# Two more input units of the second and third feed-forward blocks as seven half-size products, with the token sums, the modulation dots and their buffers moved to make room

## The chip, the cores and the metric

One core of one Trainium2 chip runs the whole program. The metric is the device time of one execution in microseconds (us), median over runs. TensorE (PE) multiplies matrices, with its weight loads shown on a row of their own (PEld); VectorE (DVE) and ScalarE (ACT) do the elementwise work; SyncE (SP) issues the loads from memory (DMA). Each engine works through its own list of instructions in the order in which the list stands, and waits at an instruction whose data or buffer isn't ready.

## The reference, cut to what matters

A two-layer model on 256 latent and 256 context tokens (512 in all), width 1024. Each layer is: half feed-forward block (FFN), mixer (attention in layer 0, mLSTM in layer 1), half FFN. Scale, shift and gate of each block come from a vector of conditions:

```python
mod = split(silu(c) @ ada_w[i] + ada_b[i], 9)      # once with c, once with c_ctx
def half_ffn(h, shift, scale, gate, w_in, w_out, g, b):
    xm = h * (1 + scale) + shift
    a, u = split(xm @ w_in, 2)                     # 1024 -> 2 x 2816
    y = (silu(a) * u) @ w_out                      # 2816 -> 1024
    return layer_norm(alpha * h + 0.5 * gate * y, g, b)
```

All of it is in 32-bit floating point.

## The kernel before, in words

**Products.** A product of two fp32 numbers is made of three matmuls on operands that are cut in a high and a low part (`mm3`, L241): high·high, high·low, low·high. The cut is `split`: ACT casts the high part (L225), DVE subtracts it from the whole to leave the low part (L230). Weights arrive whole by DMA (512 KB a tile of 128x1024, line L210, three buffers called raw) and are split into one of seven buffers, each a pair of high and low.

**FFNs.** There are four. The first stands before attention, the second after it, the third right after the second, the last after mLSTM. The first three go through `ffn`: the 2816 inner columns are 22 units of 128, in two halves of 11. In each half the input units come first (`unit_in`: 8 blocks of width, both a and u, three matmuls of 512 tokens each, so 48 matmuls), then the 8 output rows (`unit_out`: 11 units by three matmuls of 512 tokens, 33 in all), whose result DVE adds onto h (L713). Units 0 to 3 are done for the two halves of the tokens apart (lead units); so are the last four rows of the second half (tail).

**Fast units.** In the second and third FFN the second half's units 11 to 21 use a Strassen-like scheme (`fast_in`): a product of 2x2 blocks by seven half-size products in place of eight. The weight blocks of a unit are a11, a21 (first tile) and a12, a22 (second tile); the weight sums are s1 = a21 + a22, s2 = s1 - a11 and so on (four DVE additions and subtractions on 128x512, L636, then splits). The token blocks are the lower and upper half of the width by latent and context tokens; their sums are made once by `fast_sums` and overwrite the context part of the operand in place. The seven products (each 4 blocks by three matmuls of 256 tokens, so 84 matmuls a unit) are a11, a12, s1, s2, a22, s4, s3 in the order of the code; ACT copies partial results out of PSUM in between (L661 to L668), DVE combines them (L670, L674, L675), ACT applies silu (L671).

**Side work.** The vectors mod are dots of silu(c) with the columns of ada_w. DVE does them beside the matmuls: one piece is a tile of 128x1024 (512 KB) and one instruction for each of two condition vectors (`ada_dot`, L350). A call after each unit or row first does the dots of pieces that were loaded at the call before, then loads new ones. Layer normalisation leaves a scaling of h to be finished beside the units (`residual`, L563 and L564). In the program before, 56 pieces are done in the first FFN; the rest in the units 0 to 10, in the first rows and in the second half's rows of the second and third FFN. The token sums stand beside rows 4 and 5 of the first half, when the buffers of the dots have been closed to make room; silu(c) is loaded and computed again after unit 21.

**Order.** A scheduler gives each engine its list when the kernel is built; what stands where is read from that list.

Of the kernel before, what the change touches and what calls it, by code (L numbers as in the profile page):

```python
# [9 lines left out]
F32 = mybir.dt.float32  # L10
# [4 lines left out]
ALU = mybir.AluOpType  # L15
# [18 lines left out]
SH = 16  # L34
SHM = 48
SHR = 56
# [19 lines left out]
LEAD = 4  # L56
# [6 lines left out]
S1B = 5  # L63
# [18 lines left out]
FAFTER = 2  # L82
# [7 lines left out]
SUMSAT = 4  # L90
FLIP = 56
PIECES = 4
DOTS = {
    1: {**{("in", j): 2 for j in range(11)}, **{("out", 0, d): 2 if d < 2 else 1 for d in range(4)}, **{("out", 1, d): 1 for d in range(4)}},
    2: {**{("in", j): 2 for j in range(4)}, **{("in", j): 3 if j < 9 else 2 for j in range(4, 11)}, **{("out", 0, d): 2 if d < 3 else 0 for d in range(4)},
        **{("out", 1, d): 2 if d < 3 else 1 for d in range(4)}},
}
# [75 lines left out]
class Body:  # L173
    def __init__(self, ctx, tc, a, out):
        self.tc, self.nc, self.a, self.out = tc, tc.nc, a, out
        self.n = 0
        self.sp = ctx.enter_context(tc.tile_pool(name="sp", bufs=1))
        self.pp = ctx.enter_context(tc.tile_pool(name="pp", bufs=1, space=PSUM))
        self.later, self.running = [], []
        self.fence = {}  # L180
        self.fine = False

        self.nraw, self.spare = 0, None

# [104 lines left out]
    def silu_c(self):  # L289

        pool = ExitStack()
        self.n += 1
        p = pool.enter_context(self.tc.tile_pool(name=f"cp{self.n}", bufs=1, side="right"))
        self.cp = p
        self.cb = self.t([P, 2, D], pool=p)
        return pool
# [5 lines left out]
    def silu_all(self):  # L302
        pool = self.silu_c()
        self.silu_load()
        self.silu()
        return pool
# [285 lines left out]
    def fast_operands(self, st):  # L592

        n = ND // 2 * TL
        x = self.t([P, 6 * n], F32R, pool=st)
        self.t([P, FLIP], pool=st)
        self.made = [[x[:, (2 * i + p) * n : (2 * i + p + 1) * n].rearrange("p (k f) -> p k f", f=TL) for p in range(2)] for i in range(3)]

    def fast_sums(self, i):
# [5 lines left out]
        def at(ks, g):  # L605
            return self.xh[:, ks, g[0] : g[1]], self.xl[:, ks, g[0] : g[1]]

        def whole(ks, g):
            o = self.tmp().rearrange("p (k f) -> p k f", k=2)
            h, l = at(ks, g)  # L610
            V.tensor_tensor(out=o, in0=h.bitcast(F32), in1=l.bitcast(F32), op=ALU.add)
            return o

        a, b = whole(lo, LAT), whole(lo, CTX)
        V.tensor_tensor(out=a, in0=a, in1=b, op=ALU.subtract)
        self.split(a, *at(lo, CTX))
# [3 lines left out]
        V.scalar_tensor_tensor(a, a, -1.0, c, ALU.mult, ALU.subtract)  # L620
        self.split(a, *made(0))
        d = whole(up, LAT)
        V.scalar_tensor_tensor(d, a, -1.0, d, ALU.mult, ALU.subtract)
        self.split(d, *made(2))

    def fast_in(self, j, w_in, st):

        nc, V, S = self.nc, self.nc.vector, self.nc.scalar
        half = 4 * P
        t4 = self.made[2]  # L630
# [5 lines left out]
        add = lambda o, x, y: V.tensor_tensor(out=o, in0=x, in1=y, op=ALU.add)  # L636
        ws = [self.pair(sh=SHR if j == NFH else SH, n=half)] + [self.pair(sh=SH) for _ in range(3)]
# [6 lines left out]
        self.split(sums[:, : 2 * half], *ws[2])  # L644
        self.split(sums[:, 2 * half :], *ws[3])
# [21 lines left out]
        product(z, "a22", lambda k: [x[:, k, :] for x in t4], True, True)  # L667
# [11 lines left out]
    def ffn(self, layer, s, gate, groups, side, start=None, cpool=None):  # L679
# [4 lines left out]
        with self.tc.tile_pool(name=f"ffn{li}", bufs=1) as gp:  # L684
# [34 lines left out]
            for hf in range(2):  # L719
# [21 lines left out]
                fast = cpool is not None and hf == 1  # L741
                for j in js:
                    if fast:
                        self.fast_in(j, w_in, st)
                        continue
                    unit_in(j, stream(j), allg)
                    assert not self.running
                    if j >= LEAD + FAFTER:
                        self.fine = False
                    call("in", j)  # L750
# [5 lines left out]
                if fast:  # L756
                    more.close()
                    cpool = self.silu_all()
                for d in range(body):
                    if cpool and not hf and d == SUMSAT:  # L760
                        self.flush()
                        cpool.close()
                        self.n += 1
                        more = ExitStack()
                        st = more.enter_context(self.tc.tile_pool(name=f"st{self.n}", bufs=1, side="right"))
                        self.fast_operands(st)
                    unit_out(hf, d, w, allg)
                    if cpool and not hf and d >= SUMSAT and d - SUMSAT < 2:
                        self.fast_sums(d - SUMSAT)
                    call("out", hf, d)  # L770
                if body < ND:
                    w = Keep(self, w.chunks, SH, w)
                    self.fine = True
                    for g in groups:
                        for d in range(body, ND):
                            unit_out(hf, d, w, g, TAILSTEP)
                    self.steps('B')
        return cpool
# [846 lines left out]
def emit(ctx, tc, a, out):  # L1625
# [4 lines left out]
    cpool = b.silu_c()  # L1630
    both2 = (0, 1)
    queue = [(0, p, both2) for p in range(16, 72)]
    later = [(1, p, both2) for p in range(40)] + [(1, p, (0,)) for p in range(40, 72)]
    made = {}

    def once(key, f):
        def get():
            if key not in made:
                made[key] = f()
            return made[key]  # L1640
        return get

    def side(key, coef, keep=(True, True), nxt=True, alone=False, dots={}):
        def pop():
            for _ in range(3 if len(queue) > 40 else 2):
                if queue:
                    b.ada(*queue.pop(0))

        def some(n):
            b.flush()  # L1650
            for _ in range(min(n, len(later))):
                layer, dt, vecs = later.pop(0)
                b.waiting.append((b.ada_load(layer, dt), layer, dt, vecs))

        get = once(key, coef)

        b.begin = lambda g: b.norm(g, get, keep[0 if g == LAT else 1], nxt, alone)
        s = {}
        for j in range(NF):
            s["in", j] = (lambda j=j: some(dots.get(("in", j), 0))) if dots else pop  # L1660
        for d in range(ND):
            s["out", 0, d] = (lambda d=d: some(dots.get(("out", 0, d), 0))) if dots else pop
            s["out", 1, d] = lambda d=d: some(dots.get(("out", 1, d), 0))
        return s

    both = (LAT, CTX)
    b.ffn(0, 0, once("g0", lambda: b.half_gate(0, 2)), both, side("n0", lambda: b.ln_mod(0, 0, (0, 3))), start)
    assert not queue
    cpool.close()
    b.attention(lambda: b.shift_(0, 5), side("n1", lambda: b.ln_mod(0, 1, (0, 6))))  # L1670
    cpool = b.silu_all()
    cpool = b.ffn(0, 1, once("g1", lambda: b.half_gate(0, 8)), both, side("n2", lambda: b.ln_mod(0, 2, (1, 0)), dots=DOTS[1]), cpool=cpool)
    cpool = b.ffn(1, 0, once("g2", lambda: b.half_gate(1, 2)), both, side("n3", lambda: b.ln_mod(1, 0, (1, 3)), (True, False), dots=DOTS[2]), cpool=cpool)
    assert not later, len(later)
    b.flush()
    cpool.close()
# [96 lines left out]
```

## Time and profile before

| | |
|---|---|
| median of three runs | 1624.87 us (1624.43 to 1624.98) |
| the profiled execution's own time | 1623.31 us |
| its span in the trace | 1621.5 us |
| PE busy | 1606.1 us, 99% of the span |
| PEld busy | 1448.6 us |
| DVE busy | 1351.5 us, 83% |
| ACT busy | 744.6 us, 46% |
| granted TensorE clock | 0.998 of full speed |
| read from memory | 248.79 MB |

Of the stages that matter here, in the second FFN: units 4 to 10 end at about 678 us of the span, the eight rows follow until 739 us, units 11 to 21 until 844 us. In the third FFN units 11 to 21 fill 1094 to 1194 us. A busy time is the time in which an engine has an instruction in work; instructions of PE and DVE overlap the one before by a little, so where they stand back to back their starts are closer than their durations. "Idle before" names the engine that ended the wait.

### The profile page before, as it was taken

What the parts mean: (1) busy time and instruction counts of PE and PEld (TensorE: products, weight loads), DVE (VectorE), ACT (ScalarE), POOL (GpSimd) and SP (SyncE); (2) the same over time, 40 slices, a digit from 0 to 9 for tenths busy, and PEclk for the clock granted to TensorE, in tenths of its full rate; (3) what the DMA queues carried; (4) which work ended last, traced back from release to release, by engine and by line L of the source; (5) the groups of instructions that cost most, each with busy time, mean ns of one, the idle gap of its engine ahead of it and who ended that gap; (6) DMA issues with size and microseconds to landing.
All of it is one profiled execution on the core that took longest, in us unless ns stands there. A gap on an engine that the chain in (4) does not pass through costs nothing. (4 is left out here: it accounts for less than half of the span.)

```text
span 1621.5 us, 26548 instructions
## 1 busy us (share of the span) xinstructions
PE 1606.1 (99%) x10280; PEld 1448.6 (89%) x10280; DVE 1351.5 (83%) x2687; ACT 744.6 (46%) x1268; POOL 62.8 (4%) x77
## 2 busy tenths in 40 slices
PE   9999999999999999999999999999999999999998
PEld 7888888889988998889998998889999989999987
DVE  7899978648879879999976979699967968897687
ACT  6522132314676443325662433336642657566542
POOL 0000000001011200000000100000001000020000
PEclk9999999999999999999999999999999999999999
DMA  9677765422202347733354258723362342438552
GB/s 358 221 249 237 239 205 186 139 69 85 66 1 94 141 143 218 219 110 124 111 164 162 79 177 290 248 65 105 107 237 87 98 130 92 145 103 257 179 176 91
DMA packets 72222, 251.56 MB, mean 155 GB/s; under 512 B 7960, under 2 KB 10776, under 8 KB 72096
## 3 DMA queue, kind: packets, MB, share of 16 engines
q1 hardware_dynamic: 71520, 249.09, 47.8%
q8 instruction: 80, 1.31, 0.3%
q10 hardware_dynamic: 576, 0.79, 0.1%
q14 instruction: 46, 0.38, 0.1%
HBM read 248.79 MB, written 1.05 MB: 154 GB/s over the span
## 5 line engine op out<-in xcount | busy, mean ns | idle before, releaser
L241 PE MATMUL t<-t,t 128*128 128x256 f32 (+2 forms) x8340 | 1305.0, 317 | 3.7 <-ACT t L541 1.1
L241 PEld LDWEIGHTS t<-t,t 128*128 128x128 f32 x8340 | 1173.1, 188 | 121.4 <-DVE t L542 1.9
L225 ACT CAST t<-t 128x1024 fp32r<-128x1024 f32 (+3 forms) x509 | 422.8, 850 | 478.1 <-PE t L241 236.1
L230 DVE TENSOR_TENSOR t<-t,t 128x256 fp32r<-128x256 f32 (+2 forms) x728 | 506.2, 730 | 110.5 <-ACT t L225 107.4
L350 DVE SCALAR_TENSOR_TENSOR t<-t,t 128x1024 bf16<-128x1024 f32 x224 | 260.8, 1222 | 0.0
L588 ACT ACTIVATE t<-t 128x512 f32<-128x512 f32 (+1 forms) x71 | 34.4, 490 | 100.7 <-PE t L241 99.7
L931 PE MATMUL t<-t,t 128*128 128x256 f32 (+1 forms) x256 | 79.6, 311 | 0.2 <-ACT t L541 0.2
L933 PE MATMUL t<-t,t 128*128 128x256 f32 (+1 forms) x256 | 78.8, 308 | 0.1
L932 PE MATMUL t<-t,t 128*128 128x256 f32 (+1 forms) x256 | 78.7, 307 | 0.1
L713 DVE SCALAR_TENSOR_TENSOR t<-t,t,t 128x256 f32<-128x256 f32 x96 | 42.9, 481 | 40.5 <-PE t L241 40.5
L589 DVE TENSOR_TENSOR t<-t,t 128x512 f32<-128x512 f32 (+1 forms) x71 | 39.1, 554 | 40.7 <-PE t L241 27.6
L484 POOL TENSOR_TENSOR t<-t,t 128x256 f32<-128x256 f32 x30 | 23.6, 786 | 1103.4 <-ACT t L474 1101.9
L859 PE MATMUL t<-t,t 128*128 128x512 f32 (+1 forms) x300 | 60.5, 364 | 0.0
L859 PEld LDWEIGHTS t<-t,t 128*128 128x128 f32 x300 | 51.5, 189 | 8.9
L1460 PE MATMUL t<-t,t 128*128 128x512 f32 (+2 forms) x276 | 55.4, 356 | 0.3 <-ACT t L1545 0.3
L474 ACT ACTIVATE t<-t 128x256 f32<-128x256 f32 x72 | 26.2, 412 | 64.0 <-DVE t L467 64.0
L1460 PEld LDWEIGHTS t<-t,t 128*128 128x128 f32 (+1 forms) x276 | 44.9, 183 | 11.1 <-ACT t L1545 0.7
L931 PEld LDWEIGHTS t<-t,t 128*128 128x128 f32 x256 | 48.4, 189 | 3.2 <-ACT t L541 0.4
L932 PEld LDWEIGHTS t<-t,t 128*128 128x128 f32 x256 | 48.1, 188 | 3.3 <-DVE t L230 0.8
L933 PEld LDWEIGHTS t<-t,t 128*128 128x128 f32 x256 | 48.1, 188 | 2.8 <-DVE t L542 0.3
L541 ACT ACTIVATE t<-t,t 128x256 fp32r<-128x256 f32 x72 | 32.8, 502 | 31.2 <-DVE t L540 31.2
L636 DVE TENSOR_TENSOR t<-t,t 128x512 f32<-128x512 f32 x66 | 45.5, 689 | 0.9 <-DVE t L230 0.3
(209 smaller groups left out, 1104.3 us busy)
## 6 DMA issues: line engine op xcount, KB each, us to landing
t<-in_ffn_in SPq DMA_DIRECT2D x168, 512.0 KB, 4.1
t<-in_ada_w SPq DMA_DIRECT2D x138, 512.0 KB, 4.2
t<-in_ffn_out SPq DMA_DIRECT2D x66, 512.0 KB, 4.4
t<-in_ffn_last SPq DMA_DIRECT2D x22, 512.0 KB, 3.6
t<-in_att_in SPq DMA_DIRECT2D x12, 512.0 KB, 3.4
t<-in_att_out SPq DMA_DIRECT2D x8, 512.0 KB, 3.6
t<-in_ml_qk SPq DMA_DIRECT2D x8, 512.0 KB, 3.9
t<-in_ml_v SPq DMA_DIRECT2D x8, 512.0 KB, 3.5
```

What stands on the lines that cost most here:

```text
L225: self.behind(self.nc.scalar.copy(h, x))
L230: self.behind(self.nc.vector.tensor_tensor(out=ls, in0=xs, in1=hs.bitcast(F32), op=ALU.subtract))
L241: mm = lambda *k, **kw: self.nc.tensor.matmul(*k, skip_group_check=not group, **kw)
L350: ins = nc.vector.scalar_tensor_tensor(self.tmp().bitcast(BF16), r, 1.0, self.cb[:, v, :], ALU.mult, ALU.mult, accum_out=to)
L589: V.tensor_tensor(out=sl, in0=sl, in1=pu[:, :n], op=ALU.mult)
L636: add = lambda o, x, y: V.tensor_tensor(out=o, in0=x, in1=y, op=ALU.add)
L713: V.scalar_tensor_tensor(z, y[:, gg[0] - t0 : gg[1] - t0], gate()[:, v, d : d + 1], z, ALU.mult, ALU.add)
L859: pin(nc.tensor.matmul(o, gs[g], ws[k][w][:, i : i + n], start=k == k0 and g == w == 0, stop=k == k1 - 1 and g == 1,))
L931: mm(o, self.xh[:, k, c], wh, start=k == 0, stop=False)
L932: mm(o, self.xh[:, k, c], wl, start=False, stop=False)
L933: mm(o, self.xl[:, k, c], wh, start=False, stop=k == ND - 1)
L1460: mm = lambda *k, **kw: pin(nc.tensor.matmul(*k, **kw))
```

## The change

1. In the second and third FFN units 9 and 10 are done by `fast_in` too, so 13 fast units each in place of 11.
2. The token sums are therefore made earlier: `fast_operands` and the two calls of `fast_sums` stand beside units 5 and 6. The sum that overwrites the context tokens is kept aside (`first`) and written by four splits after unit 8 (`fast_first`). The buffers of the dot pieces are closed at unit 5.
3. A fast unit's weight sums are four buffers of 512 columns, split by four splits of 128x512, in place of two splits of 128x1024.
4. The dots: 64 pieces in the first FFN in place of 56; in the second and third, pieces in the lead units, then two (second) or three (third) pieces in each of the eight rows of the first half and some in the second half's rows; none in units 4 to 21. As their own buffers are closed by then, the pieces of the rows are loaded into halves of the seven weight pairs. The pieces loaded at row 7 are used in row 0 of the second half.
5. A tail row does the dots that are still waiting; `residual` is also called in units 9 and 10.
6. silu(c) keeps a buffer of its own, so it isn't loaded and computed again after unit 21 (four small DMAs and four ACT instructions in all).

```diff
-SUMSAT = 4
+FAST = {0: (99, 99), 1: (9, 5), 2: (9, 5)}
 DOTS = {
-    1: {**{("in", j): 2 for j in range(11)}, **{("out", 0, d): 2 if d < 2 else 1 for d in range(4)}, **{("out", 1, d): 1 for d in range(4)}},
...
+    0: {**{("in", j): 3 if j < 16 else 2 for j in range(4, 21)}, **{("out", 0, d): 2 for d in range(8)}, ("out", 1, 0): 1, ("out", 1, 1): 1},
+    1: {**{("in", j): 2 for j in range(3)}, **{("out", 0, d): 2 for d in range(8)}, **{("out", 1, d): 1 for d in range(4)}},
+    2: {**{("in", j): 2 for j in range(3)}, **{("out", 0, d): 3 for d in range(8)}, **{("out", 1, d): 2 for d in range(4)}},
 }
...
-        r = self.t([P, 1024], tag="ada", bufs=PIECES, pool=self.cp)
+        if self.cp:
+            r = self.t([P, 1024], tag="ada", bufs=PIECES, pool=self.cp)
+        else:
+            self.halves = self.halves or self.pair(F32)
+            r = self.halves.pop()
...
+    def fast_first(self):
+        for k in range(ND // 2):
+            self.split(self.first[k], *self.x(k, CTX))
...
-        sums = self.t([P, 4 * half], tag="sums", bufs=1, pool=st)
-        s1, s2, s4, s3 = (part(sums, i) for i in range(4))
+        s1, s2, s4, s3 = (self.tmp() for _ in range(4))
...
-        self.split(sums[:, : 2 * half], *ws[2])
-        self.split(sums[:, 2 * half :], *ws[3])
+        for i, x in enumerate((s1, s2, s4, s3)):
+            self.split(x, *(part(y, i % 2) for y in ws[2 + i // 2]))
...
-                fast = cpool is not None and hf == 1
+                fast, sums = FAST[li]
                 for j in js:
-                    if fast:
-                        self.fast_in(j, w_in, st)
-                        continue
-                    unit_in(j, stream(j), allg)
...
+                    if j >= fast:
+                        self.fast_in(j, w_in, SHR if j in (fast, NFH) else SH)
+                    else:
+                        unit_in(j, stream(j), allg)
...
+                    if j <= sums:
+                        call("in", j)
                     self.residual(2, self.pin)
+                    if j == sums:
+                        self.fast_operands()
+                    if sums <= j < sums + 2:
+                        self.fast_sums(j - sums)
+                    if j == fast - 1:
+                        self.fast_first()
```

**How the orders change.** On DVE before, at the passage from row 7 of the second FFN's first half to unit 11 (L713 is the row's result; t1208 the weight sums of unit 11, t1211 and t1212 their low parts; t1222 to t1226 belong to unit 12):

```order
L636 TENSOR_TENSOR t1208_7091<-t1208_7091,t1206_7087 128x512
L636 TENSOR_TENSOR t1208_7091<-t1206_7087 128x512
L636 TENSOR_TENSOR t1208_7091<-t1208_7091,t1207_7089 128x512
L230 TENSOR_TENSOR t1211_7094<-t1208_7091,t1211_7094 128x1024
L230 TENSOR_TENSOR t1212_7095<-t1208_7091,t1212_7095 128x1024
L230 TENSOR_TENSOR t1223_7214<-t1220_7209,t1223_7214 128x512
L636 TENSOR_TENSOR t1222_7213<-t1220_7209,t1221_7211 128x512
L636 TENSOR_TENSOR t1222_7213<-t1220_7209 128x512
L713 SCALAR_TENSOR_TENSOR t2_66<-t1203_7046,t1146_6694,t2_66 128x256 x2
L230 TENSOR_TENSOR t1224_7215<-t1221_7211,t1224_7215 128x1024
```

All of unit 11's sums and low parts, and part of unit 12's, stand ahead of row 7's result. The same place on DVE now (L359 is a dot, L728 the result of row 7, t1224 is s1, t1225 s2 and t1226 s4 of unit 11, t1230 the pair of high and low parts of s1 and s2):

```order
L359 SCALAR_TENSOR_TENSOR t1211_7167,t1204_7118<-t1205_7119,t963_5447 128x1024
L359 SCALAR_TENSOR_TENSOR t1212_7169,t1204_7118<-t1205_7119,t963_5447 128x1024
L728 SCALAR_TENSOR_TENSOR t2_66<-t1214_7174,t1158_6842,t2_66 128x256 x2
L359 SCALAR_TENSOR_TENSOR t1217_7215,t1204_7118<-t1213_7171,t963_5447 128x1024
L359 SCALAR_TENSOR_TENSOR t1218_7217,t1204_7118<-t1213_7171,t963_5447 128x1024
L359 SCALAR_TENSOR_TENSOR t1219_7219,t1204_7118<-t1213_7171,t963_5447 128x1024
L359 SCALAR_TENSOR_TENSOR t1220_7221,t1204_7118<-t1213_7171,t963_5447 128x1024
L651 TENSOR_TENSOR t1224_7230<-t1222_7226,t1223_7228 128x512
L651 TENSOR_TENSOR t1225_7231<-t1224_7230,t1222_7226 128x512
L231 TENSOR_TENSOR t1230_7236<-t1224_7230,t1230_7236 128x512
L651 TENSOR_TENSOR t1226_7232<-t1225_7231,t1223_7228 128x512
L651 TENSOR_TENSOR t1227_7233<-t1222_7226 128x512
```

The four dots of the pieces loaded at row 6 stand behind row 7's result, and every weight sum of unit 11 stands behind them. In the third FFN the same place has three dots there.

On PE, the first products of unit 11 in the second FFN now (t1229 holds a12 and a22, t1230 s1 and s2; the row of 12 is the product a22):

```order
L242 MATMUL t1233_7255<-t4_68,t1229_7235 128x256
L242 MATMUL t1233_7255<-t3_67,t1229_7235 128x256
L242 MATMUL t1234_7256<-t1078_6255,t1229_7235 128x256 x12
L242 MATMUL t1233_7255<-t3_67,t1230_7236 128x256
L242 MATMUL t1233_7255<-t4_68,t1230_7236 128x256
L242 MATMUL t1233_7255<-t3_67,t1230_7236 128x256 x2
```

The product a22 was fifth, behind s1 and s2; it is now third, so 36 matmuls (a11, a12, a22) stand ahead of the first that needs s1.

On DVE now, the new fast unit 10 of the second FFN, from its first weight's low part (t1142) on (t1138 is s1 and t1137 the second weight tile of unit 10, t1132 and t1133 the results of unit 9, t1144 the low parts of s1 and s2):

```order
L231 TENSOR_TENSOR t1142_6669<-t1136_6661,t1142_6669 128x512
L651 TENSOR_TENSOR t1138_6665<-t1136_6661,t1137_6663 128x512
L651 TENSOR_TENSOR t1139_6666<-t1138_6665,t1136_6661 128x512
L231 TENSOR_TENSOR t1143_6670<-t1137_6663,t1143_6670 128x1024
L685 TENSOR_TENSOR t1132_6559<-t1132_6559,t1130_6557 128x512
L689 SCALAR_TENSOR_TENSOR t1133_6560<-t1129_6556,t1133_6560 128x512
L651 TENSOR_TENSOR t1140_6667<-t1139_6666,t1137_6663 128x512
L690 TENSOR_TENSOR t1132_6559<-t1132_6559,t1133_6560 128x512
L651 TENSOR_TENSOR t1141_6668<-t1136_6661 128x512
L231 TENSOR_TENSOR t1144_6671<-t1138_6665,t1144_6671 128x512
L231 TENSOR_TENSOR t1144_6671<-t1139_6666,t1144_6671 128x512
```

These rows are new: unit 10 was an ordinary unit. Between the addition that makes s1, the first instruction that needs the second weight tile, and the low part of s1 stand seven others.

More of the change, by code (lines that the diff above doesn't have):

```diff
@@ L603, in fast_sums @@
         made = lambda k: [x[:, lo, :] for x in self.made[k]]
[L605 to L606 removed]
         def whole(ks, g):
             o = self.tmp().rearrange("p (k f) -> p k f", k=2)
[L610 to L611 removed]
+            h, l = (x[:, ks, g[0] : g[1]].bitcast(F32) for x in (self.xh, self.xl))
+            V.tensor_tensor(out=o, in0=h, in1=l, op=ALU.add)
             return o
         a, b = whole(lo, LAT), whole(lo, CTX)
[L615 to L616 removed]
+        for k in range(2):
+            o = self.first[2 * i + k] = self.t([P, TL], tag="s1", bufs=S1B)
+            V.tensor_tensor(out=o, in0=a[:, k, :], in1=b[:, k, :], op=ALU.subtract)
         c = whole(up, CTX)
@@ L666, in fast_in @@
         S.copy(a[:, TL:], x)
-        product(z, "a22", lambda k: [x[:, k, :] for x in t4], True, True)
+        product(z, "a22", made(2), True, True)
         S.copy(u[:, :TL], z)
@@ L677, in fast_in, with ffn @@
         self.split(a, gh, gl)
-    def ffn(self, layer, s, gate, groups, side, start=None, cpool=None):
+    def ffn(self, layer, s, gate, groups, side, start=None):
         nc, V = self.nc, self.nc.vector
@@ L755, in ffn @@
                 body = ND - TAIL if hf else ND
-                if fast:
-                    more.close()
-                    cpool = self.silu_all()
+                self.halves = []
+                if hf and fast < NF:
+                    self.shut()
+                    self.cp = self.open()
                 for d in range(body):
[L760 to L766, printed above, removed]
                     unit_out(hf, d, w, allg)
-                    if cpool and not hf and d >= SUMSAT and d - SUMSAT < 2:
-                        self.fast_sums(d - SUMSAT)
                     call("out", hf, d)
+                self.halves = []
                 if body < ND:
@@ L1629, in emit @@
     b.setup_rest()
-    cpool = b.silu_c()
+    b.silu_c()
     both2 = (0, 1)
@@ L1643, in side @@
     def side(key, coef, keep=(True, True), nxt=True, alone=False, dots={}):
[L1644 to L1647, printed above, removed]
         def some(n):
             b.flush()
-            for _ in range(min(n, len(later))):
-                layer, dt, vecs = later.pop(0)
+            todo = queue or later
+            for _ in range(min(n, len(todo))):
+                layer, dt, vecs = todo.pop(0)
                 b.waiting.append((b.ada_load(layer, dt), layer, dt, vecs))
```

69 lines of the change are left out of this document (39 added, 30 removed).

## The prediction

> **What bounds the kernel now.** First the head of the page, and from the windows view the stages of the second FFN (units 4 to 10, the eight rows, units 11 to 21) and the fast units of the third.
>
> ```profile
> PE 1606.1 (99%) x10280; PEld 1448.6 (89%) x10280; DVE 1351.5 (83%) x2687; ACT 744.6 (46%) x1268; POOL 62.8 (4%) x77
> ```
>
> ```profile
> core 0: us, PE busy (x) PEld busy (x) DVE busy (x) ACT busy (x) POOL busy (x), PEclk, DMA share, GB/s
> 602.00:679.00 77.00, 77.00 (x345) 63.88 (x345) 71.80 (x120) 27.83 (x41) 0.00 (x0) 1.00 0.73 225
> 679.00:739.00 60.00, 60.00 (x268) 49.70 (x266) 59.42 (x103) 17.01 (x23) 0.00 (x0) 1.00 0.39 123
> 739.00:844.00 105.00, 105.00 (x927) 104.91 (x926) 97.14 (x127) 66.08 (x109) 0.00 (x0) 1.00 0.39 122
> 1094.00:1194.00 100.00, 100.00 (x885) 100.00 (x884) 91.20 (x121) 63.58 (x106) 0.00 (x0) 1.00 0.38 118
> ```
>
> PE is busy in the whole of each stage at a granted clock of 1.00, so the end moves by what PE gains in matmuls and loses in new waits, and by nothing else. DVE is second: full in the rows (59.42 of 60) and 93% in the fast units. That no product waits in the second FFN is also what the timeline of PE says, one row without idle time over 311 us:
>
> ```profile
> 574.58 311.53 PE L241 MATMUL t<-t,t 128*128 128x256 f32 x2005
> ```
>
> **The gain: units 9 and 10.** An ordinary unit ends with ACT's silu of its result, released by PE; a fast unit with DVE's first combination. Their timelines:
>
> ```profile
> 656.67 0.60 ACT L588 ACTIVATE t<-t 128x512 f32<-128x512 f32 x1 [1.20 <-PE t L241]
> 667.55 0.60 ACT L588 ACTIVATE t<-t 128x512 f32<-128x512 f32 x1 [1.32 <-PE t L241]
> ```
>
> ```profile
> 776.86 0.68 DVE L670 TENSOR_TENSOR t<-t,t 128x512 f32<-128x512 f32 x1
> 786.38 0.68 DVE L670 TENSOR_TENSOR t<-t,t 128x512 f32<-128x512 f32 x1
> ```
>
> An ordinary unit takes 10.88 us, 226.7 ns for each of 48 matmuls; a fast one 9.52, 113.3 ns for each of 84. Four units gain 4 x 1.36 = **5.44 us**. The Trainium skill, "TensorE: Matmul & The Clock Gate", section "Back-to-back issue gap", speaks against this: it gives a sustained spacing of some 131 ns at 512 columns and 81 ns at 128, so that a half-size product costs more than half; with an estimated 98 ns midway, a fast unit would be 84 x 98 - 48 x 131 = 1.9 us longer and the four units 7.8 us a loss. The trace disagrees with it, since here half the columns take half the time.
>
> **The cost: unit 11 of both FFNs.** Dots, splits, sums and row results on DVE and ACT, first by groups over the whole trace, then in the timeline of DVE at a row of the second FFN and at the passage to unit 11:
>
> ```profile
> L350 DVE SCALAR_TENSOR_TENSOR t<-t,t 128x1024 bf16<-128x1024 f32 x224 | 260.8, 1222 | 0.0
> L225 ACT CAST t<-t 128x512 fp32r<-128x512 f32 x133 | 81.8, 620 | 57.3 <-PE t L241 11.7 <-DVE t L623 8.4 <-DVE t L615 8.3
> L230 DVE TENSOR_TENSOR t<-t,t 128x512 fp32r<-128x512 f32 x133 | 91.0, 688 | 5.1 <-ACT t L225 4.7
> L636 DVE TENSOR_TENSOR t<-t,t 128x512 f32<-128x512 f32 x66 | 45.5, 689 | 0.9 <-DVE t L230 0.3
> ```
>
> ```profile
> 701.58 0.88 DVE L713 SCALAR_TENSOR_TENSOR t<-t,t,t 128x256 f32<-128x256 f32 x2
> 702.37 1.22 DVE L350 SCALAR_TENSOR_TENSOR t<-t,t 128x1024 bf16<-128x1024 f32 x1
> ...
> 706.95 1.23 DVE L230 TENSOR_TENSOR t<-t,t 128x1024 fp32r<-128x1024 f32 x1
> ```
>
> ```profile
> 737.78 0.69 DVE L636 TENSOR_TENSOR t<-t,t 128x512 f32<-128x512 f32 x1
> 738.38 0.68 DVE L636 TENSOR_TENSOR t<-t 128x512 f32<-128x512 f32 x1
> 738.99 0.87 DVE L713 SCALAR_TENSOR_TENSOR t<-t,t,t 128x256 f32<-128x256 f32 x2
> ```
>
> Four dots run from 702.37 to 706.95, 1.15 us each start to start; a 512-wide instruction starts 0.60 after the one before; a row's result takes 0.79. Before, the sums of unit 11 were made by the time of row 7's result (737.78 against 738.99). Now that result and four dots stand ahead of them on DVE.
>
> Let row 7 end on PE at 0, in the second FFN. The row's result starts at 0.08, dots run from 0.87 to 5.45, s1 is added by 6.14 (0.69), its high part cast by 6.76 (0.62). PE has by then done a11, a12 and a22, 36 matmuls, until 36 x 0.1133 = 4.08: a wait of 2.68. Two matmuls later, at 6.99, it needs the low part; DVE takes s2's addition first and has the low part at 6.76 + 0.69 = 7.45, a wait of 0.46. The other ten of s1 end at 8.58, two of s2 at 8.81; DVE meanwhile adds s4 and s3 and has s2's low part at 9.25, a wait of 0.44. That is **3.58 us**. In the third FFN three dots stand there, all is 1.15 earlier, and only the first wait shrinks: **2.43 us**. Nothing hides either, since PE's list is fixed. I take both as they are; the bounds are 0 (if the scheduler's list were not what binds) and 1 us more each for the copies of PSUM that ACT does in between.
>
> **Unit 12.** Its second weight tile is loaded into the raw buffer that the addition of s4 of unit 11 frees. That addition ends at 7.96 to 8.05 instead of well ahead. From the trace, the loads of this stage:
>
> ```profile
> DMA to landing us min/median/max: 3.4/3.7/4.9
> ```
>
> So it lands at 11.75. Behind it on DVE stand, until s1's low part is made, nine 512-wide instructions and a split of 1024 columns:
>
> ```profile
> 739.77 1.22 DVE L230 TENSOR_TENSOR t<-t,t 128x1024 fp32r<-128x1024 f32 x1
> 740.90 1.42 DVE L636 TENSOR_TENSOR t<-t,t 128x512 f32<-128x512 f32 x2
> ```
>
> That is 9 x 0.60 + 1.13 = 6.5, so s1's low part is there at 18.3. Unit 11 ends at 9.52 + 3.58 = 13.1, and PE reaches that part after a11, a12, two of s1 and a22, at 17.4. I take **0.95 us** for each FFN; 0 if the load comes at 3.4 and DVE runs without a gap, 2 if it takes 4.9.
>
> **Units 9 and 10.** The weight sums of unit 9 stand beside unit 8's result: from the end of unit 8, DVE does that result, s2, s1's low part, the result's own low part, two residuals (0.79), s4, s3, then s2's low part, which is ready at 5.2; PE needs it at 4.99, a wait of 0.2. The addition of s4 ends at 4.0, so the second tile of unit 10 lands at 7.7, and by the list in the section on the change s1's low part follows eight 512-wide instructions and one split of 1024 later, at 13.7; PE needs it at 13.1: 0.6. Then ACT's copy of the first product stands behind a cast of output weights (1024 columns) and those of s4, s3 and the unit's result, 0.3 more. **1.1 us** in each FFN; bounds 0.2 and 2.
>
> **What costs nothing.** The token sums beside units 5 and 6 cover themselves: before, units 4 to 10 left DVE 5.2 of 77 us idle, but with two or three pieces a unit, some 4.6 us each, which are gone there. The splits of `fast_first` need the lead units' context operand, which PE has left at the end of unit 8; unit 9 first reads it with s1, 2.72 us in, and the s1 copies are ready far ahead. Units 4 to 15 of the first FFN now do three pieces each, six dots of 1.15, beside two splits of 1024 and two 512-wide instructions: 10.4 us in 10.88. The rows of the third FFN (33 x 0.2267 = 7.48 us) load 3 dot pieces and 1.4 weight tiles of 0.52 MB each, 307 GB/s; the page's strip, in 40 slices, starts at 358:
>
> ```profile
> GB/s 358 221 249 237 239 205 186 139 69 85 66 1 94 141 143 218 219 110 124 111 164 162 79 177 290 248 65 105 107 237 87 98 130 92 145 103 257 179 176 91
> ```
>
> The reload of silu(c) after unit 21 held nobody up, since PE shows no wait in that stage; its going brings nothing. If one of these covers fails, the price is up to a unit's lack, some 2 us.
>
> **Sum.** -5.44 + 3.58 + 2.43 + 2 x 0.95 + 2 x 1.1 = **+4.7 us**. The profiled execution itself took 1623.31 us, so 1628.0 of that kind; the median of the runs is 1.56 above it, and against that median it is **1629.5 us**.
>
> **Rivals.** (a) *The dots don't bind.* If the pieces are dotted in time, because PE reaches row 7 later than DVE or the sums slip ahead, only the matmuls count: 1624.87 - 5.44 = 1619.4, faster. For it: DVE has 6 to 9% of idle time in the fast units. Against it: the idle time lies behind unit 11, and the list is fixed. The point from which it decides is the number of dots n behind row 7: 0.87 + 1.15 n + 0.69 + 0.62 against 4.08, so n under 1.7; there are four and three.
> (b) *Only unit 11 waits.* If units 9, 10 and 12 have their tiles in time: -5.44 + 6.01 = +0.6, 1625.4, no change. For it: those terms rest on a load of 3.7 us and an order of casts on ACT that I walked with mean durations.
> (c) *Weight pairs run short.* The pieces loaded at row 7 hold one (second FFN) or two (third) of the seven weight pairs until row 0 of the second half, so units 11 to 21 run with six or five; a fast unit uses four. If each of the third FFN's eleven units waits 0.5 us for a pair, 5.5 us come on top: 1635.0. Against it: each pair is free as soon as its product is done, and s1's pair, free at 5.4 us into a unit, has 6.8 us until the next unit's s1.
> (d) *DVE saturates.* It had 8.8 of 9.52 us of work in a fast unit (97.14 of 105); four splits of 512 at 0.60 for two of 1024 at 1.13 add 0.14. That still fits, so I give it no time of its own.
>
> **How the numbers follow.** The measurement can tell about 0.2% from no change, 3.25 us: faster is under 1621.6, slower over 1628.1. My forecast gets 0.52, of which 0.06 falls under 1628.1; (a) 0.12, almost all of it faster; (b), with cases in which half of the waits vanish, 0.22, no change; (c) 0.14, slower. So 0.11 faster, 0.29 no change, 0.60 slower. The range goes from 1623.0, which holds most of (b), to 1634.5, which holds the upper bounds of the unknown terms and part of (c).
>
> **What would show it.** In the trace after: PE idle before the first matmul of s1 in unit 11, released by ACT's cast, of about 2.7 us in the second FFN and 1.5 in the third, each with two more waits of under half a us released by DVE's splits; four and three dots between row 7's result and the first weight sum; unit-to-unit times of 9.5 us for units 9 and 10. If PE shows no wait at unit 11, (a) holds and the step that the dots bind is wrong; if it waits in every unit from 13 on, (c) or (d).

## The result, and the profile after

The changed kernel takes 1633.7 us (median of six runs, 1631.69 to 1638.02) against 1624.14 (six runs, 1623.02 to 1624.98): ratio 1.0063, 95% interval 1.0047 to 1.0079, so it is slower, by 9.6 us at the medians. Its profiled execution took 1631.98 us with a span of 1630.2, 8.7 us over that of before.

The head of the page of after, and the windows view of the same stages (units 4 to 10, rows, units 11 to 21 of the second FFN; units 11 to 21 of the third):

```profile
PE 1608.5 (99%) x10424; PEld 1456.4 (89%) x10424; DVE 1376.7 (84%) x2783; ACT 757.1 (46%) x1344; POOL 62.4 (4%) x77
...
602.00:679.00 77.00, 76.81 (x419) 66.68 (x418) 66.46 (x112) 35.41 (x64) 0.00 (x0) 1.00 0.32 105
679.00:739.00 60.00, 60.00 (x279) 50.16 (x277) 49.51 (x89) 11.13 (x13) 0.00 (x0) 1.00 0.57 199
739.00:849.00 110.00, 106.67 (x898) 105.56 (x897) 104.71 (x159) 70.77 (x133) 0.00 (x0) 0.98 0.36 120
1094.00:1200.00 106.00, 103.85 (x902) 102.87 (x902) 102.93 (x158) 67.21 (x130) 0.00 (x0) 1.00 0.32 111
```

PE has 144 matmuls more, as four units of 84 in place of 48 have to give. What was full is no longer: PE is idle for 3.3 and 2.2 us in the stages of units 11 to 21, and in the second FFN's the clock is 0.98. The rows have no wait.

Two marks on PE, the first matmuls of the sums over tokens that close the block before and the block itself, bound each FFN (between the second's end and the third's start lie about 38.3 us in both kernels). In the timeline of before they start at:

```profile
574.23 0.70 PE L447 MATMUL t<-t,t 128*128 128x256 f32 x2
...
886.01 0.70 PE L447 MATMUL t<-t,t 128*128 128x256 f32 x2
...
924.29 0.70 PE L447 MATMUL t<-t,t 128*128 128x256 f32 x2 [0.60 <-DVE t L510]
...
1237.13 0.70 PE L447 MATMUL t<-t,t 128*128 128x256 f32 x2
```

and in that of after:

```profile
573.63 0.62 PE L456 MATMUL t<-t,t 128*128 128x256 f32 x2
...
892.07 0.70 PE L456 MATMUL t<-t,t 128*128 128x256 f32 x2
...
930.42 0.70 PE L456 MATMUL t<-t,t 128*128 128x256 f32 x2 [0.30 <-DVE t L519]
...
1245.49 0.70 PE L456 MATMUL t<-t,t 128*128 128x256 f32 x2
```

The second FFN went from 311.78 to 318.44 us, the third from 312.84 to 315.07: 6.66 and 2.23 more, which is all of the 8.7. Each has gained 2.72 in matmuls, so 9.4 and 5.0 us were lost there.

Where: the timeline of PE at unit 11 of the second and of the third FFN, with the wait ahead of each row in brackets.

```profile
743.27 0.50 PE L242 MATMUL t<-t,t 128*128 128x256 f32 x2 [2.75 <-ACT t L226]
744.00 13.20 PE L242 MATMUL t<-t,t 128*128 128x256 f32 x94 [0.23 <-DVE t L231]
...
1100.55 0.50 PE L242 MATMUL t<-t,t 128*128 128x256 f32 x2 [1.54 <-ACT t L226]
1101.28 1.65 PE L242 MATMUL t<-t,t 128*128 128x256 f32 x12 [0.23 <-DVE t L231]
1103.08 7.32 PE L242 MATMUL t<-t,t 128*128 128x256 f32 x62 [0.16 <-DVE t L231]
1110.63 4.61 PE L242 MATMUL t<-t,t 128*128 128x256 f32 x37 [0.23 <-ACT t L676]
```

First a long wait for the cast of s1's high part, two matmuls, and a short wait for its low part; in the third FFN another for s2's. On DVE of after, behind row 7, stand the four dots (L359, each with a short read of its result behind it), and only then the sums (L651):

```profile
737.23 1.21 DVE L359 SCALAR_TENSOR_TENSOR t<-t,t 128x1024 bf16<-128x1024 f32 x1
738.37 0.08 DVE L359 DVE_READ_ACCUMULATOR t<-t,t 128x1 f32 x1
738.37 1.22 DVE L359 SCALAR_TENSOR_TENSOR t<-t,t 128x1024 bf16<-128x1024 f32 x1
739.52 0.08 DVE L359 DVE_READ_ACCUMULATOR t<-t,t 128x1 f32 x1
739.52 1.22 DVE L359 SCALAR_TENSOR_TENSOR t<-t,t 128x1024 bf16<-128x1024 f32 x1
740.66 0.08 DVE L359 DVE_READ_ACCUMULATOR t<-t,t 128x1 f32 x1
740.66 1.22 DVE L359 SCALAR_TENSOR_TENSOR t<-t,t 128x1024 bf16<-128x1024 f32 x1
741.81 0.08 DVE L359 DVE_READ_ACCUMULATOR t<-t,t 128x1 f32 x1
741.81 1.41 DVE L651 TENSOR_TENSOR t<-t,t 128x512 f32<-128x512 f32 x2
743.25 0.69 DVE L231 TENSOR_TENSOR t<-t,t 128x512 fp32r<-128x512 f32 x1
```

Nothing else held the sums up. Unit 11's two weight tiles were issued at 715.6 and 722.5 us and landed within 5.2 us, some 14 us ahead of the first sum at 741.81. Ahead of row 7's result DVE even stood idle for 0.90 us (1.44 in the third FFN), waiting for PE, with the dots and the sums in its list behind that result. So at this point it is the order of DVE's list that binds: what the sums need was there.

What the prediction did not have comes behind the long wait. The windows view cut at it, in the second FFN:

```profile
740.00:743.30 3.30, 0.55 (x6) 0.35 (x4) 3.23 (x7) 0.67 (x2) 0.00 (x0) 1.00 0.00 0
743.30:748.10 4.80, 4.58 (x24) 4.37 (x25) 4.38 (x8) 3.23 (x7) 0.00 (x0) 0.65 0.49 166
748.10:752.00 3.90, 3.90 (x35) 3.90 (x35) 2.75 (x4) 2.47 (x4) 0.00 (x0) 0.99 0.16 64
```

After the wait of 2.75 us the granted clock is 0.65 over 4.8 us (0.50 in its last 3.3), and matmuls start 213 ns apart: some 1.7 us lost. After the 1.54 us of the third FFN the clock stays at 1.00.

And the pace of the half-size matmuls has a second value. Groups of PE in 20 us of units 11 to 21, after, from 765 and from 820 us on:

```profile
L242 PE MATMUL t<-t,t 128*128 128x256 f32 x179 | 20.4, 276 | 0.0
...
L242 PE MATMUL t<-t,t 128*128 128x256 f32 x172 | 20.4, 281 | 0.0
```

In both PE waits for nothing and the clock is 1.00, but one has 179 matmuls and the other 172: starts 113.3 and 117.8 ns apart. In before, units 11 to 21 run at 113.3 from end to end in both FFNs; in after, the slower pace holds from 804 to 849 us, 45 us of which 3.8%, 1.7 us, is lost; it also holds from 660 us on in units 9 and 10 of the second FFN, and from 1028 us on in those of the third.

Summing starts of PE's records beyond 113.3 ns gives, for the second FFN: units 9 and 10, 1.45 us (0.8 in waits, the rest pace); unit 11, 3.5 in waits and 1.7 by the clock; unit 12, 0.3; units 16 and 17, 1.0 in waits behind ACT's copies; pace behind them 1.7. For the third: units 9 and 10, 1.4; unit 11, 2.7; unit 12, 0.6. That adds up to 9.7 and 4.7, near the 9.4 and 5.0 by the marks. A wait counts here with the wider spacing just beside it, so these figures are somewhat larger than the idle times in brackets above.

### The profile page after: what moved, and what is told of

The parts are those of the page before. It is cut to its first block, busy times and chain, and to the rows that moved or that the text cites. A ratio compares the mean times of both kernels' runs of the same rounds, so it can differ in the third digit from the quotient of the medians.

```text
span 1630.2 us, 26994 instructions
## 1 busy us (share of the span) xinstructions
PE 1608.5 (99%) x10424; PEld 1456.4 (89%) x10424; DVE 1376.7 (84%) x2783; ACT 757.1 (46%) x1344; POOL 62.4 (4%) x77
## 3 DMA queue, kind: packets, MB, share of 16 engines
HBM read 246.69 MB, written 1.05 MB: 152 GB/s over the span
## 5 line engine op out<-in xcount | busy, mean ns | idle before, releaser
L226 ACT CAST t<-t 128x1024 fp32r<-128x1024 f32 (+4 forms) x573 | 435.7, 785 | 480.1 <-PE t L242 148.9
L231 DVE TENSOR_TENSOR t<-t,t 128x256 fp32r<-128x256 f32 (+3 forms) x792 | 516.0, 689 | 98.3 <-ACT t L226 95.1
L359 DVE SCALAR_TENSOR_TENSOR t<-t,t 128x1024 bf16<-128x1024 f32 x224 | 260.4, 1220 | 0.0
L597 ACT ACTIVATE t<-t 128x256 f32<-128x256 f32 (+1 forms) x67 | 32.1, 483 | 102.3 <-PE t L242 101.2
L728 DVE SCALAR_TENSOR_TENSOR t<-t,t,t 128x256 f32<-128x256 f32 x96 | 42.6, 478 | 39.3 <-PE t L242 39.2
L598 DVE TENSOR_TENSOR t<-t,t 128x256 f32<-128x256 f32 (+1 forms) x67 | 36.2, 545 | 32.2 <-ACT t L597 19.9
L651 DVE TENSOR_TENSOR t<-t,t 128x512 f32<-128x512 f32 x78 | 53.6, 687 | 2.9 <-DMA t<-in_ffn_in 2.0
```

Source lines behind the costliest of these rows:

```text
L226: self.behind(self.nc.scalar.copy(h, x))
L231: self.behind(self.nc.vector.tensor_tensor(out=ls, in0=xs, in1=hs.bitcast(F32), op=ALU.subtract))
L359: ins = nc.vector.scalar_tensor_tensor(self.tmp().bitcast(BF16), r, 1.0, self.cb[:, v, :], ALU.mult, ALU.mult, accum_out=to)
L598: V.tensor_tensor(out=sl, in0=sl, in1=pu[:, :n], op=ALU.mult)
L728: V.scalar_tensor_tensor(z, y[:, gg[0] - t0 : gg[1] - t0], gate()[:, v, d : d + 1], z, ALU.mult, ALU.add)
```

## The experiments

Two theories at the start. D: the dots behind row 7 delay unit 11's sums, and what follows is their price. L: what binds are the landing of weight tiles and the splits of the fast units, and the dots stand where time would be lost anyway.

**No dots behind row 7.** The table of dots alone is changed:

```diff
-    1: {**{("in", j): 2 for j in range(3)}, **{("out", 0, d): 2 for d in range(8)}, **{("out", 1, d): 1 for d in range(4)}},
-    2: {**{("in", j): 2 for j in range(3)}, **{("out", 0, d): 3 for d in range(8)}, **{("out", 1, d): 2 for d in range(4)}},
+    1: {**{("in", j): 2 for j in range(4)}, **{("out", 0, d): 0 if d == 6 else 2 for d in range(8)}, **{("out", 1, d): 1 for d in range(4)}},
+    2: {**{("in", j): 3 if j == 3 else 2 for j in range(4)}, **{("out", 0, d): 0 if d == 6 else 3 for d in range(8)}, **{("out", 1, d): 2 for d in range(4)}},
```

> The kernel after, but no piece is loaded at row 6 of the second and third FFN's first half, so no dot stands between row 7's result and the weight sums of unit 11; the pieces go to the calls after the lead units. Theory D (the dots behind row 7 make unit 11 wait, and after the longer wait the clock falls to half): the waits of 3.5 and 2.7 us at unit 11 go, and so do the 1.7 us of half clock in the second FFN, some 8 us, from 1633.7 to about 1625.5; PE's timeline shows no idle time before the first product with s1 of unit 11. Theory L (what binds is the weight tiles' landing and the splits in the fast units, and the dots only stand where time would be lost anyway): the wait at unit 11 is then released by another split and the kernel stays at 1631 or above.

1621.27 us (11 runs); ratio to before 0.9986 (0.9977 to 0.9995). The timeline of PE, second and third FFN, and the windows of units 11 to 21:

```profile
670.47 213.46 PE L242 MATMUL t<-t,t 128*128 128x256 f32 x1483 [1.39 <-DVE t L231]
...
1020.31 213.69 PE L242 MATMUL t<-t,t 128*128 128x256 f32 x1483 [0.35 <-DVE t L231]
```

```profile
740.00:840.00 100.00, 100.00 (x885) 100.00 (x884) 97.11 (x145) 67.28 (x127) 0.00 (x0) 1.00 0.37 125
1095.00:1190.00 95.00, 95.00 (x841) 95.00 (x840) 91.63 (x138) 63.16 (x120) 0.00 (x0) 1.00 0.35 121
```

Behind the waits of 1.39 and 0.35 us in unit 10 there is none to the end of the FFN's units, and 885 matmuls take 100 us, the pace of before. L falls for unit 11. The kernel is 12.4 us faster than after, 4 more than D expected: the waits and the half clock account for some 8; the slower pace and the waits of units 16 and 17, which D had not charged to the dots, are gone too, some 2.7; and the median of after lies 1.7 above its profiled execution.

The edit also takes away the loads at row 6 and the weight pairs that they hold. The kernel after speaks against these as the cause: in its third FFN three pieces are loaded there and three dots stand behind row 7, in its second two pieces and four dots, and the longer wait is the second's.

**Fast from unit 11.** Against the kernel after:

```diff
-FAST = {0: (99, 99), 1: (9, 5), 2: (9, 5)}
+FAST = {0: (99, 99), 1: (11, 5), 2: (11, 5)}
```

> The kernel after with units 9 and 10 of the second and third FFN as ordinary units; sums, dots and buffers as in the kernel after. Theory D: the four fast units gain 5.44 us in matmuls and lose about 2.9 in waits and slower matmuls around them, so without them the kernel is some 2.5 us slower than the kernel after, 1636, with the waits at unit 11 unchanged. Theory L: the new fast units are the loss, and without them the kernel comes to 1629 or below.

1636.63 us (5 runs), 1.0078 (1.0066 to 1.0090) of before. Its unit 11 in the second FFN:

```profile
745.05 0.50 PE L242 MATMUL t<-t,t 128*128 128x256 f32 x2 [2.76 <-ACT t L226]
```

L's 1629 is out: the loss of 12.8 us against before lies in the rest of the change. By the medians the four new fast units are worth 2.9 us even with their waits, but that is not certain, since the runs of the two kernels overlap (1631.7 to 1638.0 for after, 1633.9 to 1636.9 here).

**Two dots.** Row 6 loads one piece in the second FFN and two in the third (one vector each), two dots behind row 7 in both.

```diff
-    1: {**{("in", j): 2 for j in range(3)}, **{("out", 0, d): 2 for d in range(8)}, **{("out", 1, d): 1 for d in range(4)}},
-    2: {**{("in", j): 2 for j in range(3)}, **{("out", 0, d): 3 for d in range(8)}, **{("out", 1, d): 2 for d in range(4)}},
+    1: {**{("in", j): 2 for j in range(3)}, ("in", 3): 1, **{("out", 0, d): 1 if d == 6 else 2 for d in range(8)}, **{("out", 1, d): 1 for d in range(4)}},
+    2: {**{("in", j): 2 for j in range(3)}, ("in", 3): 1, **{("out", 0, d): 2 if d == 6 else 3 for d in range(8)}, **{("out", 1, d): 2 for d in range(4)}},
```

> The kernel after with two dots behind row 7 in both FFNs in place of four and three. Theory D, by the sum of the prediction (0.87 + 2 x 1.15 + 0.69 + 0.62 = 4.48 against 4.08): a first wait of 0.4 us and two of 0.45 behind it at each unit 11, 1.3 us for each FFN, and no half clock, so about 1628.3. Theory L: as in the kernel without dots, 1631 or above, without an order by the number of dots.

1628.08 us (10 runs), 1.0030 (1.0018 to 1.0043). PE at the two units 11:

```profile
742.48 0.50 PE L242 MATMUL t<-t,t 128*128 128x256 f32 x2 [0.46 <-ACT t L226]
...
1098.29 0.50 PE L242 MATMUL t<-t,t 128*128 128x256 f32 x2 [0.39 <-ACT t L226]
```

The formula gave 0.40, and the wait is the same in both FFNs though one piece is loaded at row 6 in the second and two in the third: again it goes by the dots. That the median meets the expected 1628.3 is in part luck. The expectation added 1.3 us for each FFN to 1625.5 for no dots; the kernel without dots takes 1621.3, so two dots cost 6.8 us, not 2.6. The runs spread from 1624.8 to 1633.0; the profiled one, 1631.5, has the slower pace from 752 us to the end of the second FFN's units, and from 1130 in the third's.

**None in the second, four in the third.** Against the kernel without dots behind row 7:

```diff
-    2: {**{("in", j): 3 if j == 3 else 2 for j in range(4)}, **{("out", 0, d): 0 if d == 6 else 3 for d in range(8)}, **{("out", 1, d): 2 for d in range(4)}},
+    2: {**{("in", j): 2 for j in range(3)}, **{("out", 0, d): {5: 2, 6: 4}.get(d, 3) for d in range(8)}, **{("out", 1, d): 2 for d in range(4)}},
```

> No dots behind row 7 in the second FFN (as in the first kernel of these) and four in place of three in the third. If a wait of 2.7 us halves the clock for some 3 us and one of 1.5 us does not, as the kernel after shows in its second and third FFN, unit 11 of the third FFN now waits 2.7 us at first and runs 3 us at clock 0.5: 1.15 + 1.7 us more there, about 1631.2 in all. If the half clock had another cause in the second FFN, the clock stays at 1.00 and the time is about 1629.5.

1626.86 us (12 runs), 1.0024 (1.0013 to 1.0035). Unit 11 of the third FFN, timeline and windows:

```profile
1098.19 0.50 PE L242 MATMUL t<-t,t 128*128 128x256 f32 x2 [2.76 <-ACT t L226]
```

```profile
1098.30:1103.00 4.70, 4.47 (x24) 4.27 (x25) 3.92 (x7) 3.10 (x7) 0.00 (x0) 0.64 0.51 159
```

Wait and clock are as in the second FFN of after: the half clock follows the wait, not the place. The time is lower than expected because the kernel without dots was; over that one the median is 5.6 us, where 5.7 was expected. The profile can't confirm that sum: it is of the slowest of the twelve runs (1634.4), in which the third FFN took 7.3 us more than without dots, with the slower pace from 1158 us on, and the second, where no unit waited, 3.1 more.

**The pieces in the first FFN.** Against the kernel without dots behind row 7:

```diff
-    0: {**{("in", j): 3 if j < 16 else 2 for j in range(4, 21)}, **{("out", 0, d): 2 for d in range(8)}, ("out", 1, 0): 1, ("out", 1, 1): 1},
-    1: {**{("in", j): 2 for j in range(4)}, **{("out", 0, d): 0 if d == 6 else 2 for d in range(8)}, **{("out", 1, d): 1 for d in range(4)}},
-    2: {**{("in", j): 3 if j == 3 else 2 for j in range(4)}, **{("out", 0, d): 0 if d == 6 else 3 for d in range(8)}, **{("out", 1, d): 2 for d in range(4)}},
+    0: {**{("in", j): 3 for j in range(4, 21)}, **{("out", 0, d): 2 for d in range(8)}, ("out", 1, 0): 2, ("out", 1, 1): 2},
+    1: {**{("in", j): 2 for j in range(3)}, **{("out", 0, d): 0 if d == 6 else 2 for d in range(8)}, **{("out", 1, d): 1 for d in range(4)}},
+    2: {**{("in", j): 2 for j in range(3)}, **{("out", 0, d): 0 if d == 6 else 3 for d in range(8)}, **{("out", 1, d): 2 for d in range(4)}},
```

> As the kernel without dots behind row 7, but the pieces taken from row 6 go to the first FFN (three in each of units 4 to 20) and not to the calls after the lead units of the second and third. There they delayed the splits of unit 10: PE waited 1.4 us once in the second FFN, where the kernel after waited 0.1. If that wait comes from the dots before it on DVE, it goes back to some 0.3 us and the time falls by 1 to 1.5 us, to about 1620; the first FFN, at an estimated 10.4 of 10.88 us of DVE a unit, shows no wait. If the first FFN can't hold them, PE waits there and the time stays at 1621 or rises.

1621.40 us (11 runs), 0.9987 (0.9978 to 0.9997): no gain. The first FFN holds the dots without a wait, but unit 10 of the second still waits 1.38 us. DVE there, and the issue of the second weight tile on SP:

```profile
665.30 1.42 DVE L651 TENSOR_TENSOR t<-t,t 128x512 f32<-128x512 f32 x2 [1.92 <-DMA t<-in_ffn_in]
```

```profile
660.43 0.33 SPq L211 DMA_DIRECT2D t<-in_ffn_in  x1
```

The expectation is wrong: the dots do not delay that split, the tile does. Issued at 660.43 when s4's addition frees its buffer, it lands 4.9 us later. In the kernel after the same load was issued at 660.14 and landed after 3.5 us, and PE waited only 0.06. Why it took longer here is open.

**Residuals early.** On top of that, all residuals of the second and third FFN in units 4 to 7:

```diff
-                    self.residual(2, self.pin)
+                    self.residual(2 if li == 0 else 4 if j < 8 else 0, self.pin)
```

> As the one with the pieces in the first FFN, and in the second and third FFN the residuals are done four a unit in units 4 to 7, and none in units 8 to 10. By the prediction's walk two residuals (0.79 us on DVE) stand ahead of the sums s4, whose end starts the load of unit 10's second tile. If that order binds, the waits at units 9 and 10 shrink by up to 0.8 us in each FFN, and the time by 1 to 1.5 us against the one before; if the load or ACT's copies bind, it stays within 0.5 us.

1620.35 us (9 runs, 1619.22 to 1620.68), 0.9979 (0.9969 to 0.9989) of before: the fastest kernel here but for one that equals it, 13.3 us below after. DVE, SP and PE at unit 10:

```profile
663.43 1.42 DVE L651 TENSOR_TENSOR t<-t,t 128x512 f32<-128x512 f32 x2 [0.70 <-DMA t<-in_ffn_in]
```

```profile
659.78 0.33 SPq L211 DMA_DIRECT2D t<-in_ffn_in  x1
```

```profile
669.63 214.49 PE L242 MATMUL t<-t,t 128*128 128x256 f32 x1487 [0.21 <-DVE t L231]
```

Without two residuals ahead of s4 the tile is issued 0.65 us earlier; it also lands sooner, after 3.65 us, at 663.43, and PE waits 0.21. So of the 1.87 us by which the tile is there earlier, 1.2 are the load's own; in after, with the residuals in place, it took no longer. In the third FFN, where the load took 3.4 and 3.5 us, the wait at unit 10 goes from 0.22 to 0.07. The order binds as expected, but that it brought the whole 1.05 us between the medians is not shown.

**Fast from unit 8 on.** Against the kernel with early residuals:

```diff
-FAST = {0: (99, 99), 1: (9, 5), 2: (9, 5)}
+FAST = {0: (99, 99), 1: (8, 5), 2: (8, 5)}
-                    self.residual(2 if li == 0 else 4 if j < 8 else 0, self.pin)
+                    self.residual(2 if li == 0 else 6 if j < 7 else 0, self.pin)
```

> As the one with early residuals (six a unit in units 4 to 6), and unit 8 of the second and third FFN is a fast unit too. Theory D: with DVE free of dots there each further fast unit brings its 1.36 us, less up to 0.4 for slower spacing of matmuls, so 2 to 2.7 us less in all, about 1616.5. If the fast units themselves are the loss (theory L), nothing is gained or it becomes slower.

1620.72 us (11 runs), 0.9977 (0.9969 to 0.9986): as the one before, not the 2 to 2.7 us less. By what was set down beforehand this speaks for L at these units: one more fast unit loses about what it gains. In its profiled execution the second FFN is 0.1 and the third 0.6 us shorter than there, not 1.36 each: units 8 to 10, 13 and 15 of the second wait in pieces of 0.1 to 0.35 us, and the slower pace holds in part. In the one before, the first FFN and attention are also 1.2 us shorter, which the edit doesn't touch.

**One dot.** The kernel with early residuals, one dot behind row 7 of the third FFN:

```diff
-    2: {**{("in", j): 2 for j in range(3)}, **{("out", 0, d): 0 if d == 6 else 3 for d in range(8)}, **{("out", 1, d): 2 for d in range(4)}},
+    2: {**{("in", j): 2 for j in range(3)}, **{("out", 0, d): {5: 2, 6: 1}.get(d, 3) for d in range(8)}, **{("out", 1, d): 2 for d in range(4)}},
```

> As the kernel with early residuals, but one dot stands behind row 7 of the third FFN (none in the second). By the prediction's formula s1 is ready at 0.87 + 1.15 + 0.69 + 0.62 = 3.33 us, before PE reaches it at 4.08, so no wait for its cast; its low part is ready 0.7 later, at 4.02, before 4.31, and s2's low part is early too: PE shows no wait at unit 11 and the time stays within 1 us of 1620.4. If every dot behind row 7 costs its 1.15 us, the wait is 1.15 and the time about 1621.5 or, with slower spacing of the matmuls behind it, 1624.

In the profiled execution (1619.29 us) no wait stands before s1 in unit 11; the first is at unit 12, for ACT's copy:

```profile
1098.79 21.49 PE L242 MATMUL t<-t,t 128*128 128x256 f32 x186 [0.30 <-ACT t L676]
```

The median of 11 runs is 1623.37 (1619.29 to 1625.80), 0.9995 (0.9986 to 1.0004), 3.0 above the kernel with early residuals, so half of the expectation fails: the formula holds for the wait in the one execution that has a profile, but the others take up to 6.5 us more than it. It is the fastest of them and doesn't show that time. The median is near the 1624 set down for the other case, a wait of 1.15 us and slower spacing, but no such wait is in the profile; what the time is, is open.

## Why the prediction was right, and where it was off

The direction and its reason held: the matmuls gained what was said, and waits at unit 11 took it back. Point by point:

- **Unit 11, 3.58 and 2.43 us of waits.** Measured 3.5 and 2.7, with the wider spacing beside the waits. That the second FFN's sum came out so close is in part luck: its first wait was as said (2.75 for 2.68), the one for s1's low part was 0.23 in place of 0.46, and the one for s2's did not come, as PE was at half clock by then; the spacing made up for it. The first waits for 0, 1, 2, 3 and 4 dots were none, none, 0.39 to 0.46, 1.54 and 2.75 us; the formula gives none, none, 0.40, 1.55 and 2.70. This is the term on which the forecast stood, and the kernels with other numbers of dots show that it is the dots. For one dot there is a single profile, of the fastest run.
- **Units 9 and 10, 1.1 us each.** Measured 1.45 and 1.4 with the slower pace, 0.8 of it in waits in the second FFN and 1.1 in the third. The chain was the one walked (s4's addition, tile, sums): with the residuals moved the tile is issued 0.65 us earlier. How long the wait is goes by the load: 3.5 us in after, 4.9 in the kernel with the pieces in the first FFN, where PE waited 1.38 in unit 10.
- **Unit 12, 0.95 each.** Measured 0.3 and 0.6; over-sized. In the second FFN PE had by then lost time in unit 11 by the clock; why it was less in the third was not followed up.
- **The sum, +4.7 us, was too small** (+8.7 in the profiled execution, +9.6 at the medians). The terms that were mis-sized are the second FFN's: behind the wait of 2.75 us it left out 1.7 us at half clock; it took DVE's lag to be spent after unit 12, but units 16 and 17 waited 1.0 more; and it took the half-size matmul at 113.3 ns throughout, which cost 1.7 us there and 0.6 in units 9 and 10. For the third FFN 4.5 us was said and 5.0 measured. The measured time lies near the upper end of the range. The room there had been left for the bounds of the terms and for (c); what filled it was the half clock and the slower pace, which stood in no term.
- **What costs nothing** cost nothing: no wait in the first FFN, in units 5 to 8 or in the rows.
- **Rivals.** (a) is out: the list binds. (b) is out: units 9 and 10 wait as well. (c) is out: without dots the two pairs are held just the same, and no unit from 11 on waits. (d) in its plain form is out too: without dots behind row 7 DVE at 97.11 of 100 us keeps PE full. With the lag from unit 11 DVE was busy for 39.9 of the 40 us from 760 to 800 us, and units 16 and 17 waited for ACT; without the dots these waits are gone too. That DVE's lag was carried there from unit 11 is a reading of this, not shown by itself.

The Trainium skill's figures on the spacing of matmuls ("TensorE: Matmul & The Clock Gate", section "Back-to-back issue gap"), which spoke against half-size products, did not hold here: the spacing was 113.3 to 117.8 ns at 256 columns against 226.7 at 512. With the waits gone the kernel takes 0.9979 of before.

## What to carry to other kernels

Work that an engine does in the shadow of one stage is not free at the stage's last step: ask what the next stage wants from that engine in its first microseconds, and count what stands ahead of it in that engine's list (here four and three dots of 1.15 us decided between 0.6% slower and 0.1% faster than before). A wait of PE can cost more than its length, so look at the granted clock and the spacing behind it. Where a load is released by an instruction of a full engine, whatever stands ahead of that instruction delays the load.

## What the runs showed of the hardware

**Half clock after a short wait.** A first wait of 2.75 or 2.76 us was followed by a fall of the clock in each of three cases (0.65, 0.65 and 0.64 over 4.7 to 4.9 us: after, the kernel that is fast from unit 11, and the one with four dots in the third FFN); none of the six of 1.19 to 1.54 us at units 10 and 11 of these kernels was. In each of the three cases the clock was 0.50 for 3.41 us, and fell 0.6 to 1.5 us after PE had begun again. The Trainium skill, "TensorE: Matmul & The Clock Gate", section "What's actually happening", says that the clock halves after a window of about 3.4 us without work, and that the window runs free. The trace agrees with halving; the idle time that was enough is shorter, 2.75 us and, two matmuls later, 0.23 more. Three cases can't tell whether a wait of that length always halves the clock.

**Two paces of half-size matmuls.** 113.3 or 117.8 ns, at full clock and without waits. In the profiled kernels without a wait at unit 11 (before, none behind row 7, the pieces in the first FFN, early residuals) all eight stages of units 11 to 21 kept 113.3. Of the seven such stages with waits at unit 11 five ran at 117.8 for a part, and two, the third FFNs of after and of the kernel fast from unit 11, did not. The change doesn't always stand behind a wait: in the second FFN of the kernel with four dots in the third, where no unit from 11 on waited, it came at 771 us between two matmuls that started 175 ns apart, and in the third FFN of the kernel with two dots likewise at 1131 us. Eleven units at the slower pace are 11 x 84 x 4.5 ns, 4.2 us, of the size of the spread of the kernels that wait (1631.7 to 1638.0 for after, against 1619.2 to 1620.7 with early residuals). What sets it is not settled, and that it makes the spread was not shown: only one execution of each kernel has a profile.
